# An encoder block on one core: the first gate/up pair from blocks 3 and 2, its operands made during the last output products, and attention products by array halves

## The chip, the core and the metric

The kernel runs on one core of a Trainium2 chip. TensorE (PE) multiplies: it holds a stationary operand of up to 128 x 128 in its array (loaded by PEld, beside a running product) and streams a moving operand through it into PSUM. VectorE (DVE), ScalarE (ACT) and GpSimd (POOL) do the rest, and SyncE (SP) issues most of the DMAs. The metric is the device time of one execution in microseconds. Three runs of the kernel before took 2155.74, 2158.10 and 2158.45 us, median 2158.1.

## The reference

One layer of a bidirectional encoder on x (1, 2048, 1024) in float32:

```
h   = RMSNorm(x);  p = h @ w_in                     q, k, v, g, two low-rank decays, u, z
A   = chunked gated linear attention, 4 heads (dk 64, dv 128), forwards and backwards
      scores = (q*exp(b)) (k*exp(-b))^T, masked;  o = scores v + (q*exp(b)) state
      o = RMSNorm(o) per head * silu(g)
Bm  = gelu(u) * (W_s LayerNorm(gelu(z)) + b)        per 128-token chunk and channel group
x   = x + concat(A, Bm) @ w_out
x   = x + (silu(h2 @ w_gate) * (h2 @ w_up)) @ w_down,   h2 = RMSNorm(x)
out = RMSNorm(x)
```

The hidden width of the last product is 2816, which is 22 tiles of 128.

## The kernel before, in words

The 2048 tokens are four blocks of 512 (b = 0 to 3). Every wide product is done in three passes: each float32 operand is split into a rounded part "h" (an ACT cast) and the remainder "l" (a DVE subtraction), and PE does h·h, h·l and l·h (L112 to L114, and L873 to L875). The small products of the attention are plain float32, each of which is two matmuls in the trace.

The stages in order of time. (1) Forward over blocks 0 to 3: projections of q, k and v, and the attention of the block before, put between those products. For each 128-token chunk `attend` makes the scores `sc` (L483: 8 products with contraction 64; first four for the heads in rows 0 to 63, then four for rows 64 to 127), transposes `kp`, the output `po` (four products with the masked scores, L512, and two with the state, L519, whose moving operand is a 128 x 256 state with zeros in the quarters that belong to the other head) and the state's increment `pd` (L527). (2) Backward over blocks 3 to 0: z, gate and u products, the backward attention `pob` (L693, again two products with a zero-filled 128 x 256 state), and the eight output products `pout`, whose sums become the block's residual stream x. While the next block's products run, `settle` and `norm2` turn x into h2 in place; blocks 3 and 2 are written to DRAM (`d_h`). (3) Gate and up products. Two blocks of tokens make a pair, and two tiles of hidden channels a set; each 2 x 2 product of a set is done with seven products of half the size instead of eight (Strassen-Winograd). Products 0 to 6 use seven moving operands held in `slots`, made by `moving` out of the pair's four quarters (b11, b21 of the first block and b12, b22 of the second) by `sub` (L237) and `put` (cast L226, remainder L227), and seven stationary operands, made for each set by `Stationary.job` out of two weight tiles (loads L302, sums L313, cast L334, remainder L335). `PAIRS` gives the pairs: (1, 0), then (3, 2). The gate's values go through a tanh into `cg`, the up products times `cg` go to DRAM (`d_a`). (4) The down products, block by block, and the last norm.

Engines run their queues in order; which instruction stands where on an engine is decided by a scheduler that works from the program's order, and a tile that reuses memory waits for the last reader of what was there. Around the change this matters at three places: the pair (1, 0) needs block 0, whose x is complete only with the last output product, and whose norm (`sums.rstd`, L194 to L196, and `norm_x0`, L837) comes before three of the operands; `tb` (operands 3 and 1) takes the buffer of `y`, the moving operand of the output products; and the pool `pf` of stage 3 takes the memory of the pool `pc` of stage 2.

Of the kernel before, what the change touches and what calls it, by code (L numbers as in the profile page):

```python
# [27 lines left out]
def encoder_block(  # L28
# [34 lines left out]
    mixer = ExitStack()  # L63
    mx = mixer.enter_context(tc.tile_pool(name="mx", bufs=1))
# [100 lines left out]
    rall = mx.tile([P, NB * TT], F32, tag="rall", name="rall")  # L165
# [54 lines left out]
    slots = {}  # L220

    def put(i, src, eng=nc.vector):
        hi, lo = slots[i]
        for k in range(0, HK, 2):
            c = slice(k, k + 2)
            nc.scalar.copy(out=hi[:, c, :], in_=src[:, c, :])  # L226
            eng.tensor_tensor(out=lo[:, c, :], in0=src[:, c, :], in1=hi[:, c, :].bitcast(F32), op=ALU.subtract)  # L227

    def moving(xa, xb, early=True, normed=None):


        b11, b21, b12, b22 = xa[:, 0:HK, :], xa[:, HK:KT, :], xb[:, 0:HK, :], xb[:, HK:KT, :]

        def sub(o, a, b, eng=nc.vector):
            for k in range(0, HK, 2):
                c = slice(k, k + 2)
                eng.tensor_tensor(out=o[:, c, :], in0=a[:, c, :], in1=b[:, c, :], op=ALU.subtract)  # L237

        if early:
            put(0, b11)  # L240
        if normed:
            normed(range(0, HK))
        sub(b11, b12, b11)
        put(3, b11)
        if early:
            put(4, b21)
        if normed:
            normed(range(HK, KT))
        sub(b11, b22, b11)
        put(1, b11)  # L250
        sub(b12, b22, b12, nc.gpsimd)
        put(6, b22, nc.gpsimd)
        put(2, b12)
        sub(b21, b21, b11)
        put(5, b21)
# [4 lines left out]
    d_h = {b: drp.tile([P, KT, TB], F32, tag=f"dh{b}", name=f"dh{b}") for b in (2, 3)}  # L260
# [4 lines left out]
    ech = mx.tile([P, 4, NB * TT * 2], F32, tag="ech", name="ech")  # L265
    dec = mx.tile([P, 4, NB * TT], F32, tag="dec", name="dec")
    gnh = mx.tile([P, 4], F32, tag="gnh", name="gnh")
# [8 lines left out]
    PAIRS = ((1, 0), (3, 2))  # L276
    TURNS = (0, NF // 2 - 1)
    STEADY = (0, 3, 4, 1, 2, 5, 6)

    class Stationary:  # L280


        def __init__(self):
            self.pool, self.n, self.two = None, 0, None
            sets = [(pair[0], p, which) for pair in PAIRS for p in range(NF // 2) for which in range(2)]
            self.made = [dict(of=s) for s in sets]

            jobs = []
            for i in range(0, len(sets), 2):
                jobs += ([(i + j, o) for o in STEADY for j in range(2)] if sets[i][1] in TURNS else  # L290
                         [(i + j, o) for j in range(2) for o in STEADY])
            self.stream = Stream([lambda j=j: self.job(*j) for j in jobs], ahead=4)

        def raw(self, i, r):
            if i < len(self.made) and r not in self.made[i]:
                b, p, which = self.made[i]["of"]
                name = f"w{'gu'[which]}{b}_{p}{'ab'[r]}"
                if (r == 0) if i < 2 else i % 2 == 0:
                    t = wp.tile([P, D], F32, tag="wraw", name=name, bufs=2)
                else:  # L300
                    t = self.pool.tile([P, D], F32, tag="raw", name=name, bufs=2)
                nc.sync.dma_start(out=t, in_=wgu[2 * p + r, which])  # L302
                self.made[i][r] = t
            return self.made[i].get(r) if i < len(self.made) else None

        def job(self, i, o):
            m = self.made[i]
            c1, c2 = slice(0, TB), slice(TB, D)
            ra = self.raw(i, 0)
            rb = self.raw(i, 1) if o not in (0, 4) else None  # L310
# [5 lines left out]
            if o == 3:  # L316
                m["s"] = self.pool.tile([P, TB], F32, tag="sum", name=f"sum{i}", bufs=2)
                src = into(m["s"], rb[:, c1], rb[:, c2], ALU.add)
            elif o == 1:
                src = into(m["s"], m["s"], ra[:, c1])  # L320
            elif o == 2:
                src = into(rb[:, c1], ra[:, c1], rb[:, c1])
            elif o == 6:
                src = into(m["s"], ra[:, c2], m["s"])
            else:
                src = {0: ra[:, c1], 4: ra[:, c2]}[o] if o != 5 else rb[:, c2]
            if o == 2:
                self.raw(i + 1, 0)
                self.raw(i + 1, 1)
# [5 lines left out]
            nc.vector.tensor_tensor(out=lo, in0=src, in1=hi.bitcast(F32), op=ALU.subtract)  # L335
            return hi, lo
# [4 lines left out]
    with tc.tile_pool(name="pa", bufs=1) as pa:  # L341
# [84 lines left out]
        sfs = [pa.tile([P, 2, 2, P], F32, tag=f"sf{i}", name=f"sf{i}") for i in range(2)]  # L426
        la = pa.tile([P, 2 * TT, 65], F32, tag="la", name="la")
        for z in (sfz, sbz, *sfs, la):
            nc.gpsimd.memset(z, 0.0)
# [44 lines left out]
        def attend(b, qd, kd, vs):  # L474
            for t in range(TT):
# [33 lines left out]
                po = small(f"po{g}")  # L509
                sf, sn = sfs[g % 2], sfs[(g + 1) % 2]  # L510
                for hd in range(4):
                    nc.tensor.matmul(out=po[:, hd * P:(hd + 1) * P], lhsT=s[:, hd, :], rhs=vs[t][:, hd, :],  # L512
                                     start=hd == 0, stop=g == 0 and hd == 3)
                if g > 0:
# [7 lines left out]
                nc.scalar.copy(out=ot, in_=po)  # L522
# [9 lines left out]
                if g + 1 < NB * TT:  # L532
                    for m in range(2):
                        for a in range(2):
                            r = slice(a * 64, (a + 1) * 64)
                            if g == 0:
                                nc.vector.tensor_copy(out=sn[r, m, a, :], in_=dsb[r, 2 * m + a, :])
                            else:
                                nc.vector.scalar_tensor_tensor(  # L539
                                    out=sn[r, m, a, :], in0=sf[r, m, a, :], scalar=dec[r, m, g:g + 1], in1=dsb[r, 2 * m + a, :],  # L540
# [69 lines left out]
    gfs = load([P, KT], gf, "gfs")  # L610
    with tc.tile_pool(name="pc", bufs=1) as pc:
# [22 lines left out]
        sbs = [pc.tile([P, 2, 2, P], F32, tag=f"sb{i}", name=f"sb{i}") for i in range(2)]  # L634
        for z in sbs:
            nc.gpsimd.memset(z, 0.0)
# [13 lines left out]
        def settle(b, xt):  # L650
# [4 lines left out]
            if b > 1:  # L655
# [4 lines left out]
        for b in range(NB - 1, -1, -1):  # L660
# [17 lines left out]
            def backward():  # L678
                for t in range(TT - 1, -1, -1):
# [6 lines left out]
                    if g < NB * TT - 1:  # L686
# [4 lines left out]
                        po = small(f"pob{g}")  # L691
                        for m in range(2):
                            nc.tensor.matmul(out=po[:, 2 * m * P:2 * (m + 1) * P], lhsT=qb[:, m, :],  # L693
                                             rhs=sb[:, m, :, :].rearrange("p a v -> p (a v)"), start=m == 0, stop=m == 1)
                        nc.vector.tensor_tensor(out=o, in0=po, in1=o, op=ALU.add)  # L695
                    for m in range(2):
                        for a in range(2):
                            r = slice(a * 64, (a + 1) * 64)
# [463 lines left out]
```

## Time and profile before

| | |
|---|---|
| three runs, median | 2158.1 us |
| profiled execution | 2151.09 us, span 2149.4 us |
| PE busy | 2092.1 us, 97% of the span, 9608 matmuls |
| PEld / DVE / ACT / POOL busy | 80% / 64% / 40% / 9% |
| mean granted clock of TensorE | 0.992 |
| DMA | 275.11 MB, mean 128 GB/s |

PE is busy nearly everywhere, so the time is the sum of its matmuls plus the places where it waits. The page's row of tenths finds these places; a table by windows sizes them, and the list of waits names what PE waited for. Starts and windows are in us from the start of the span. A matmul's duration is longer than its share of the time, since matmuls are pipelined: what one costs in a row is the distance from start to start.

### The profile page before, as it was taken

The page shows a single profiled execution, that of the slowest core. Times are in us where ns is not written, and L with a number is a line of the kernel's source. Part 1 is how long each engine was busy: PE and PEld are TensorE (multiplying, and loading weights), DVE is VectorE, ACT ScalarE, POOL GpSimd, SP SyncE. Part 2 cuts the span into 40 slices and gives each one's busy share as a digit, 9 for nine tenths or more (in the row PEclk, how much of TensorE's full clock was granted, in tenths as well). Part 3 has the DMA queues.
Part 4 walks back from the last instruction along what each step waited for, and adds up shares of the span by engine and source line. Part 5 has one row for each costly group of instructions (what it writes and reads, how often), then busy time and mean ns, then how long its engine had stood idle before and what let it go on. Part 6 is the DMA issues. An engine that isn't in the chain of part 4 may idle for free. (4 is left out here: it accounts for less than half of the span.)

```text
span 2149.4 us, 25584 instructions
## 1 busy us (share of the span) xinstructions
PE 2092.1 (97%) x9608; PEld 1726.4 (80%) x9608; DVE 1385.1 (64%) x2143; ACT 868.0 (40%) x1459; POOL 198.3 (9%) x276
## 2 busy tenths in 40 slices
PE   8999999999999968999999999999999999999998
PEld 6788887888888856888888878888888888888887
DVE  5977567676767668666666986666666445363633
ACT  6755455464636433323223433232324333333321
POOL 0122223010110120000000210000000000000000
PEclk9999999999999988999999999999999999999999
DMA  7633335353543324222222242222124537454531
GB/s 264 206 126 124 98 110 179 130 194 118 172 155 115 98 85 157 79 87 71 84 93 79 74 162 83 94 79 90 67 84 160 202 109 244 157 200 157 181 113 40
DMA packets 92812, 275.11 MB, mean 128 GB/s; under 512 B 11536, under 2 KB 19600, under 8 KB 90128
## 3 DMA queue, kind: packets, MB, share of 16 engines
q1 hardware_dynamic: 78960, 223.14, 31.2%
q0 software_dynamic: 13728, 50.34, 6.4%
q8 instruction: 75, 1.23, 0.2%
q14 instruction: 49, 0.40, 0.1%
HBM read 221.01 MB, written 52.43 MB: 127 GB/s over the span
## 5 line engine op out<-in xcount | busy, mean ns | idle before, releaser
L930 POOL DMA_DIRECT2D da<-q x88 | 47.6, 541 | 778.0 <-DVE q L929 759.0
L917 ACT ACTIVATE th<-cg 128x512 f32<-128x512 f32 x66 | 41.7, 632 | 140.0 <-DVE cg L915 130.0
L918 DVE SCALAR_TENSOR_TENSOR cg<-th,cg 128x512 f32<-128x512 f32 x66 | 45.5, 689 | 28.2 <-ACT th L917 28.0
L800 DVE TENSOR_TENSOR xc<-pout,xc 128x512 f32<-128x512 f32 x32 | 22.0, 689 | 49.9 <-PE pout L114 49.9
L929 DVE SCALAR_TENSOR_TENSOR q<-q,cg 128x512 f32<-128x512 f32 x66 | 47.4, 718 | 0.0
L995 POOL DMA_DIRECT2D out_dram<-xg x12 | 8.6, 716 | 368.4 <-DVE xg L992 367.8
L517 POOL TENSOR_SCALAR qs<-QK,ech 128x128 f32<-128x128 f32 x30 | 26.2, 876 | 162.4 <-PE po L519 84.4
L702 DVE SCALAR_TENSOR_TENSOR sb<-sb,dec,dsr 64x128 f32<-64x128 f32 x60 | 21.0, 350 | 28.6 <-PE pob L693 27.5
L539 DVE SCALAR_TENSOR_TENSOR sf<-sf,dec,dsb 64x128 f32<-64x128 f32 x56 | 19.5, 349 | 24.1 <-ACT dsb L529 23.4
L483 PEld LDWEIGHTS sc<-QK 64*128 64x128 f32 x256 | 24.5, 187 | 6.4 <-issue 4.9
L483 PE MATMUL sc<-QK 64*128 64x128 f32 x256 | 27.7, 285 | 0.8 <-DVE QK L469 0.8
L980 ACT CAST a_8h<-ar 128x512 fp32r<-128x512 f32 x32 | 18.7, 618 | 21.0 <-DMA ar<-da 20.9
L690 POOL TENSOR_SCALAR qb<-qb,ech 128x128 f32<-128x128 f32 x30 | 20.5, 691 | 72.5 <-DMA qb<-dq 71.6
L707 ACT ACTIVATE junk<-o 128x128 f32<-128x128 f32 x64 | 20.0, 312 | 16.0 <-DVE o L695 10.3
L522 ACT COPY ot<-po 128x512 f32<-128x512 f32 x16 | 9.4, 586 | 40.8 <-issue 23.9
L1067 DVE TENSOR_TENSOR xg<-pd,xg 128x256 f32<-128x256 f32 x16 | 6.8, 424 | 28.2 <-PE pd L114 27.8
L1039 DVE TENSOR_TENSOR xg<-pd,xg 128x512 f32<-128x512 f32 x24 | 16.6, 690 | 12.2 <-PE pd L114 12.2
L1069 ACT ACTIVATE lsq<-xg 128x256 f32<-128x256 f32 x16 | 6.7, 417 | 40.9 <-DVE xg L1067 40.9
L875 PE MATMUL g_0c<-tbh,op2l 128*128 128x512 f32 x4 | 2.6, 654 | 20.6 <-DVE op2l L335 20.6
L981 DVE TENSOR_TENSOR a_8l<-ar,a_8h 128x512 fp32r<-128x512 f32 x32 | 20.8, 680 | 2.6 <-ACT a_8h L980 2.5
L512 PEld LDWEIGHTS po<-v,s 128*128 128x128 f32 x128 | 15.6, 191 | 8.4 <-issue 8.2
L981 DVE TENSOR_TENSOR a_0l<-ar,a_0h 128x512 fp32r<-128x512 f32 x32 | 20.8, 686 | 2.0 <-ACT a_0h L980 1.8
(3826 smaller groups left out, 7392.5 us busy)
## 6 DMA issues: line engine op xcount, KB each, us to landing
wdn<-in_wdn_dram SPq DMA_DIRECT2D x88, 512.0 KB, 3.5
da<-q POOLq DMA_DIRECT2D x88, 256.0 KB, 2.5
ar<-da SPq DMA_DIRECT2D x88, 256.0 KB, 4.0
wo<-in_wo_dram SPq DMA_DIRECT2D x32, 512.0 KB, 3.6
wqk<-in_wqk_dram SPq DMA_DIRECT2D x16, 512.0 KB, 4.0
xk<-in_xtok_dram SPq DMA_DIRECT2D x16, 512.0 KB, 5.2
wv<-in_wv_dram SPq DMA_DIRECT2D x16, 512.0 KB, 3.5
xc<-in_xT_dram SPq DMA_DIRECT2D x4, 2048.0 KB, 9.6
```

Of the source, the lines that this page charges most:

```text
L483: nc.tensor.matmul(out=sc[a][:, i // 2, i % 2, :], lhsT=kd[i][r, c], rhs=qd[i][r, c], start=True, stop=True)
L517: nc.gpsimd.tensor_scalar_mul(qs[:, m, :], qd[m][:, c], ech[:, m, 2 * g:2 * g + 1])
L539: nc.vector.scalar_tensor_tensor(out=sn[r, m, a, :], in0=sf[r, m, a, :], scalar=dec[r, m, g:g + 1], in1=dsb[r, 2 * m + a, :], op0=ALU.mult ...
L690: nc.gpsimd.tensor_scalar_mul(qb[:, m, :], qb[:, m, :], ech[:, 2 + m, 2 * g + 1:2 * g + 2])
L702: nc.vector.scalar_tensor_tensor(out=sn[r, m, a, :], in0=sb[r, m, a, :], scalar=dec[r, 2 + m, g:g + 1], in1=ds_[r, m, :], op0=ALU.mult, op ...
L707: nc.scalar.activation(out=junk, in_=o[:, hd * P:(hd + 1) * P], func=AF.Square, scale=P ** -0.5, accum_out=va[:, 4 + 4 * t + hd:5 + 4 * t ...
L800: nc.vector.tensor_tensor(out=xt[:, n, :], in0=p, in1=xt[:, n, :], op=ALU.add)
L917: nc.scalar.activation(out=th, in_=a, func=AF.Tanh, scale=0.5)
L918: later.append(lambda: nc.vector.scalar_tensor_tensor(out=o, in0=th, scalar=1.0, in1=a, op0=ALU.add, op1=ALU.mult))
L929: nc.vector.scalar_tensor_tensor(out=q, in0=a, scalar=0.5, in1=cg[:, 2 * m + t, :], op0=ALU.mult, op1=ALU.mult)
L930: nc.gpsimd.dma_start(out=d_a[pair[t]][2 * p + m], in_=q)
L981: nc.vector.tensor_tensor(out=lo, in0=raw, in1=hi.bitcast(F32), op=ALU.subtract)
```

## The change

The pairs become (3, 2) and (1, 0). Blocks 3, 2 and now 1 go through DRAM as h2. During block 0's u products and output products block 3 is loaded into the buffer that block 1 had, and block 2 into a pool of its own (`ps6`); `moving`, now a generator of 22 steps of one cast and one subtraction, or of one subtraction, all on ACT and DVE and none on POOL, does 8 steps between the output products, and one after each of the first 14 gate/up products. Block 1 is loaded when operands 5 and 6 of the first pair are done, and block 0 gets its norm in set 3 of the first pair. The second pair's 22 steps begin after the first product of the first pair's last set. The order of the products in a set is 0, 4, 3, 1, 2, 6, 5, and a pair begins with products 0 and 4 of four sets (gate and up of the first two tile pairs), which need the first block's halves alone, and no sums of weights. The weight tiles are asked for by a list of first and last uses.

In the attention the score products alternate between rows 0 to 63 and rows 64 to 127. The state has no zero quarters any more: the products of `po` and `pob` with it are four of contraction 64 with 128 columns, alternating between the halves, and write to two PSUM tiles, one for each half, which two copies or two additions read.

```diff
-    PAIRS = ((1, 0), (3, 2))
-    TURNS = (0, NF // 2 - 1)
-    STEADY = (0, 3, 4, 1, 2, 5, 6)
+    PAIRS = ((3, 2), (1, 0))
+    STEADY = (0, 4, 3, 1, 2, 6, 5)
+    def sequence():
+        seq = []
+        for i in range(len(PAIRS)):
+            seq += [(i, p, w, o) for o in STEADY[:2] for p in range(2) for w in range(2)]
+            seq += [(i, p, w, o) for p in range(2) for o in STEADY[2:] for w in range(2)]
+            seq += [(i, p, w, o) for p in range(2, NP - 1) for w in range(2) for o in STEADY]
+            seq += [(i, NP - 1, w, o) for o in STEADY for w in range(2)]
+        return seq
...
-        sub(b11, b12, b11)
-        put(3, b11)
...
-        sub(b12, b22, b12, nc.gpsimd)
-        put(6, b22, nc.gpsimd)
...
+        yield from put(0, b11)
+        yield from sub(b11, b12, b11)
+        yield from put(4, b21)
+        yield from sub(b12, b22, b12)
+        yield from put(3, b11)
+        yield from sub(b11, b22, b11)
+        yield from put(1, b11)
+        yield from put(2, b12)
+        yield from put(6, b22)
+        yield from sub(b21, b21, b11)
+        yield from put(5, b21)
...
-                for a in range(2):
-                    r = slice(a * 64, (a + 1) * 64)
-                    for i in range(4):
+                for i in range(4):
+                    for a in range(2):
+                        r = slice(a * 64, (a + 1) * 64)
                         nc.tensor.matmul(out=sc[a][:, i // 2, i % 2, :], lhsT=kd[i][r, c], rhs=qd[i][r, c], start=True, stop=True)
...
-                        nc.tensor.matmul(out=po[:, 2 * m * P:2 * (m + 1) * P], lhsT=qs[:, m, :],
-                                         rhs=sf[:, m, :, :].rearrange("p a v -> p (a v)"), start=False, stop=m == 1)
+                        for a in range(2):
+                            r = slice(a * 64, (a + 1) * 64)
+                            nc.tensor.matmul(out=po[a][:, m, :], lhsT=qs[r, m, :], rhs=sf[r, m, :], start=False, stop=m == 1)
...
+                xa = xp.tile([P, KT, TB], F32, tag="x2", name="xf3")
+                xb = [ps6.tile([P, HK, TB], F32, tag=f"w{n}", name=f"xf2{n}") for n in range(2)]
...
+                operands = todo = moving(xa[:, 0:HK, :], xa[:, HK:KT, :], *xb)
...
-                drain(todo, 2)
-            drain(todo)
+                drain(todo, 2 if b else (1, 1, 1, 1, 2, 2)[n - 2])
...
-                if start:
+                whi, wlo = ws.next()
+                if start and ops.n <= 5:
+                    bank[key] = other(f"{name}{key}")
+                elif start:
                     bank[key] = psf.tile([P, TB], F32, tag="sp", name=f"{name}{key}", bufs=7)
...
+            if i == 0 and p < 2:
+                drain(operands, 1)
+            elif i == 0 and p == 2 and o == STEADY[0] and w == 0:
+                drain(operands)
+                x1 = xp.tile([P, KT, TB], F32, tag="x2", name="xf1")
+                nc.sync.dma_start(out=x1, in_=d_h[1])
+            elif i == 0 and p == 3:
+                drain(norm, 1)
+            elif n == at_end:
+                operands = moving(x1[:, 0:HK, :], x1[:, HK:KT, :], x0[:, 0:HK, :], x0[:, HK:KT, :])
+            elif n > at_end and done < 22 and (n - at_end - 1) * 0.8 >= done + 1:
+                drain(operands, 1)
+                done += 1
```

How PE's queue changes in one forward chunk (chunk 9; `sc`, `kp`, `po` and `pd` as above, `QK` the decayed q and k, `qs` the decayed q and `sf` the state). Before:

```order
L483 MATMUL sc9_0_2227<-QK_312 128x128 x4
L483 MATMUL sc9_1_2228<-QK_312 128x128 x4
L499 MATMUL kp9_2248<-ident_84,ke9_2243 128x128 x4
...
L512 MATMUL po9_2258<-v2_1_1773,s9_2241 128x128 x4
L519 MATMUL po9_2258<-sf1_305,qs9_2263 128x256 x2
L527 MATMUL pd9_2271<-v2_1_1773,kT9_2253 128x128 x4
```

The same chunk of the changed kernel (its line numbers are 24 to 26 higher):

```order
L507 MATMUL sc9_0_2254<-QK_305 128x128
L507 MATMUL sc9_1_2255<-QK_305 128x128
...
L523 MATMUL kp9_2275<-ident_81,ke9_2270 128x128 x4
...
L536 MATMUL po9_0_2285<-v2_1_1792,s9_2268 128x128
L536 MATMUL po9_1_2286<-v2_1_1792,s9_2268 128x128
...
L545 MATMUL po9_0_2285<-sf1_300,qs9_2291 128x128
L545 MATMUL po9_1_2286<-sf1_300,qs9_2291 128x128
...
L553 MATMUL pd9_2302<-v2_1_1792,kT9_2280 128x128 x4
```

The two score rows and the two state rows stand four times and twice, in turns between the halves. The `po` products with the state now lie between products that use all 128 rows.

On DVE, after the last output product (`pout0_7`), before: `r0` is block 0's norm factor, `xc0` and `xc1` the blocks' tiles, `tbl`, `s2l` and `s5l` remainders of moving operands, `op2l` the remainder of the first stationary operand of product 3.

```order
L800 TENSOR_TENSOR xc0_5386<-pout0_7_6591,xc0_5386 128x512
L186 TENSOR_TENSOR e0a_6335<-e0a_6335,e0sq7_6618 128x512
L196 RECIPROCAL r0_6621<-r0_6621 128x128 x4
L313 TENSOR_TENSOR sum0_6697<-wg1_0b_6695 128x512
L837 SCALAR_TENSOR_TENSOR xc0_5386<-xc0_5386,g2s_3005,r0_6621 128x512 x4
L237 TENSOR_TENSOR xc1_4437<-xc0_5386,xc1_4437 128x1024 x2
...
L237 TENSOR_TENSOR xc1_4437<-xc1_4437 128x1024 x2
L335 TENSOR_TENSOR op2l_6700<-sum0_6697,op2h_6699 128x512
```

The same place of the changed kernel, on DVE (`xf3`, `xf20` and `xf21` are the loaded blocks 3 and 2, `op2l` here the remainder for product 0 of the second tile pair, from the weight tile `wg0_1a`):

```order
L826 TENSOR_TENSOR xc0_5462<-pout0_7_6686,xc0_5462 128x512
L229 TENSOR_TENSOR tbl_6728<-xf3_6419,tbh_6727 128x1024
L186 TENSOR_TENSOR r0_6428<-r0_6428,e0sq7_6713 128x512
...
L239 TENSOR_TENSOR xf3_6419<-xf21_6421,xf3_6419 128x1024 x2
L229 TENSOR_TENSOR s2l_6730<-xf20_6420,s2h_6729 128x1024
L358 TENSOR_TENSOR op2l_6749<-wg0_1a_6738,op2h_6748 128x512
```

The reciprocals, the norm of block 0 and the long run of operand pieces no longer stand ahead of the first stationary remainder. What stands there now is one sum of squares (L186, the last reader of the pool that closes) and six pieces of operands, of which the second `tbl` is left out above.

## Rows read from the trace of the kernel before

**Rows 1.** The page: busy tenths of PE in 40 slices.

```profile
PE   8999999999999968999999999999999999999998
```

**Rows 2.** Windows: stretch, length, busy us (and instructions) by engine, PEclk, DMA share, GB/s.

```profile
200.00:300.00 100.00, 99.10 (x532) 82.20 (x531) 64.93 (x132) 56.46 (x108) 18.79 (x30) 1.00 0.29 96
900.00:1100.00 200.00, 200.00 (x884) 165.68 (x883) 134.27 (x212) 61.51 (x108) 10.81 (x20) 1.00 0.24 82
778.75:822.00 43.25, 17.00 (x55) 11.65 (x55) 40.35 (x38) 17.53 (x21) 12.64 (x5) 0.64 0.30 112
...
1235.00:1250.00 15.00, 11.62 (x51) 9.10 (x50) 15.00 (x15) 5.39 (x9) 5.14 (x3) 1.00 0.55 190
```

**Rows 3.** Waits of PE: line waited for, us in total, times, longest.

```profile
PE g_0c L875 <- DVE op2l L335: 20.6, 1, 20.6
...
PE g_0a L875 <- DVE op158l L335: 3.4, 1, 3.4
```

**Rows 4.** Timeline of DVE after the last output product: start, us, instruction.

```profile
783.03 3.39 DVE L196 RECIPROCAL r<-r 128x128 f32<-128x128 f32 x4 [1.94 <-ACT r L194]
...
798.81 6.65 DVE L237 TENSOR_TENSOR xc<-xc,xc 128x1024 f32<-128x1024 f32 x2
```

**Rows 5.** Timeline of PE there.

```profile
778.52 0.39 PE L114 MATMUL pout<-y0h,wo_7l 128*128 128x512 f32 x1
...
785.99 0.39 PE L875 MATMUL u_0a<-tah,op0l 128*128 128x512 f32 x1
788.19 0.50 PE L873 MATMUL g_0a<-tah,op4h 128*128 128x512 f32 x1 [1.81 <-ACT op4h L334]
...
815.08 0.80 PE L875 MATMUL g_0c<-tbh,op2l 128*128 128x512 f32 x1 [20.56 <-DVE op2l L335]
```

**Rows 6.** Windows of the granted clock around that wait.

```profile
788.00:790.00 2.00, 1.74 (x4) 0.80 (x4) 2.00 (x4) 0.66 (x2) 0.00 (x0) 0.68 0.00 0
...
815.00:819.50 4.50, 4.42 (x11) 3.49 (x12) 4.50 (x7) 1.13 (x2) 0.00 (x0) 0.51 1.02 419
```

**Rows 7.** Instructions of lines 226 and 227: minimum, median, maximum ns, first and last start.

```profile
L226 ACT CAST tah<-xf x4: 1049/1054/1056, 1195.5 to 1208.6; 128x1024 fp32r<-128x1024 f32 x4
...
L227 DVE TENSOR_TENSOR tal<-xf,tah x4: 1208/1214/1226, 1196.6 to 1215.6; 128x1024 fp32r<-128x1024 f32 x4
```

**Rows 8.** DMA issues: count, KB each, median us from issue to landing.

```profile
xf<-dh SPq DMA_DIRECT2D x2, 2048.0 KB, 8.7
...
wg_0b<-in_wgu_dram SPq DMA_DIRECT2D x2, 512.0 KB, 3.7
```

**Rows 9.** Timeline of ACT: one cast of a stationary operand.

```profile
787.00 0.62 ACT L334 CAST op2h<-sum 128x512 fp32r<-128x512 f32 x1
```

**Rows 10.** Timeline of PE, one chunk's scores.

```profile
252.91 0.39 PE L114 MATMUL pv<-wv_0h,n3l 128*128 128x512 f32 x1
253.23 1.71 PE L483 MATMUL sc<-QK 64*128 64x128 f32 x16
254.87 0.33 PE L499 MATMUL kp<-ident,ke 128*128 128x128 f32 x1
```

**Rows 11.** Weight loads of these scores in flight at 253.66 to 253.70, and at 254.00.

```profile
253.56 0.30 PEld L483 LDWEIGHTS sc<-QK 64*128 64x128 f32 x2
...
253.89 0.30 PEld L483 LDWEIGHTS sc<-QK 64*128 64x128 f32 x4
```

**Rows 12.** Timeline of PE, the same chunk's output, and a backward one.

```profile
257.88 1.13 PE L512 MATMUL po<-v,s 128*128 128x128 f32 x8
258.84 1.03 PE L519 MATMUL po<-sf,qs 128*128 128x256 f32 x4
259.71 0.50 PE L527 MATMUL pd<-v,kT 128*128 128x128 f32 x3
...
438.79 1.03 PE L693 MATMUL pob<-sb,qb 128*128 128x256 f32 x4
439.65 1.02 PE L193 MATMUL e3m<-e3a,ones 128*128 128x512 f32 x2
```

More of the change, by code (lines that the diff above doesn't have):

```diff
@@ L280, in encoder_block @@
     class Stationary:
         def __init__(self):
[L284 to L299, printed above, removed]
-                else:
[L301 to L310, printed above, removed]
+            self.pool, self.n, self.two, self.sums = None, 0, None, {}
+            self.seq = sequence()
+            self.loads, self.use = [], []
+            for n, (i, p, w, o) in enumerate(self.seq):
+                turn = p in (0, 1, NP - 1)
+                need = []
+                for r in ((0,) if o in (0, 4) else (1,) if o in (3, 5) else (0, 1)):
+                    key = (i, p, w, r, p == 1 and o in (0, 4))
+                    at = [l for l in self.loads if l["key"] == key]
+                    if not at:
+                        first = r == 0 if turn and not key[4] else False if key[4] else w == 0
+                        at = [dict(key=key, pool=not first, first=n)]
+                        self.loads += at
+                    at[0]["last"] = n
+                    need.append(at[0])
+                self.use.append(need)
@@ new lines, in __init__, with ask @@
+            self.queues = [[l for l in self.loads if l["pool"] == x] for x in (False, True)]
+            for q in self.queues:
+                for a, b in zip(q, q[2:]):
+                    assert a["last"] < b["first"]
+            self.asked = [0, 0]
+            self.stream = Stream([lambda n=n: self.job(n) for n in range(len(self.seq))], ahead=4)
+        def ask(self, done):
+            for x, q in enumerate(self.queues):
+                while self.asked[x] < len(q) and (self.asked[x] < 2 or q[self.asked[x] - 2]["last"] < done):
+                    l = q[self.asked[x]]
+                    i, p, w, r, _ = l["key"]
+                    pool, tag = (self.pool, "raw") if x else (wp, "wraw")
+                    l["tile"] = pool.tile([P, D], F32, tag=tag, name=f"w{'gu'[w]}{i}_{p}{'ab'[r]}", bufs=2)
+                    nc.sync.dma_start(out=l["tile"], in_=wgu[2 * p + r, w])
+                    self.asked[x] += 1
@@ L312, in into, with job @@
+        def job(self, n):
+            i, p, w, o = self.seq[n]
+            self.ask(n)
+            c1, c2 = slice(0, TB), slice(TB, D)
+            ra = rb = None
+            for l in self.use[n]:
+                if l["key"][3]:
+                    rb = l["tile"]
+                else:
+                    ra = l["tile"]
             def into(dst, a, b, op=ALU.subtract):
@@ L934, in encoder_block @@
         ws = ops.stream
-        for pair in PAIRS:
-            first = pair == PAIRS[0]
-            xa, xb = (x1, x0) if first else xs
-            moving(xa, xb, not first, norm_x0 if first else None)
-            for p in range(NP):
-                g, u = gate_set(p, pair), up_set(p, pair)
-                for x, i in ([(x, i) for i in STEADY for x in (g, u)] if p in TURNS else
-                             [(x, i) for x in (g, u) for i in STEADY]):
-                    x[i]()
-                if first and p == 2:
-                    xs = []
-                    for b in PAIRS[1]:
-                        xt = xp.tile([P, KT, TB], F32, tag="x2" if b % 2 else "x", name=f"xf{b}")
-                        nc.sync.dma_start(out=xt, in_=d_h[b])
-                        xs.append(xt)
+        sets = {}
+        seq = ops.seq
+        at_end = [n for n, (i, p, w, o) in enumerate(seq) if i == 0 and p == NP - 1][0]
+        norm, done = norm_x0(), 0
+        for n, (i, p, w, o) in enumerate(seq):
+            if (i, p, w) not in sets:
+                make = (gate_set, up_set)[w]
+                sets[i, p, w] = make(p, PAIRS[i])
+            sets[i, p, w][o]()
+            if i == 0 and p < 2:
[11 more added lines that the diff above has]
+                done += 1
             flush()
```

144 lines of the change are left out of this document (66 added, 78 removed).

## The prediction

> **What bounds the kernel now.** I read the page's row of tenths first: PE is at 9 nearly everywhere, and falls at the very start, in the middle (slices 14 and 15: "6" and "8") and at the end [rows 1]. So the time is PE's work and its holes. The table by windows gives the undisturbed rate: 884 matmuls in 200 us, 0.2265 us each [rows 2]. Then the middle hole: in the 43.25 us after the last output product PE has 55 matmuls [rows 2], which at 0.2265 are 12.5 us, so 31 us are lost. The list of waits names the owner of the largest part: 20.6 us for `op2l` on DVE [rows 3]. DVE's timeline shows what stands ahead of it: the four reciprocals run to 786.4, and a subtraction of operands is still at it at 805 [rows 4]; two of them take 6.65 us where a piece of this size takes 1.21 [rows 7], while POOL works on pieces of the same operands. PE's timeline shows the same from its side: two products at once, then 1.8 us, then small runs, and a restart at 815.08 [rows 5]. The clock is part of it: 0.68 and less after the first gap, 0.51 from 815 to 819.5, so eleven matmuls take 4.4 us instead of 2.5 [rows 6]; these 2 us are within the 31. A second, smaller hole stands where the pairs change: 15 us with 51 matmuls, so 3.4 us, all in one wait for `op158l` [rows 2, 3].
>
> **The change, part by part.**
>
> The large hole. Three things that filled it go: the first pair no longer needs block 0, so its sums, reciprocals and norm are off the path (set 3 has them, with DVE busy 134 of 200 us in such sets [rows 2]: 3.4 us of reciprocals [rows 4] and eight pieces of about 0.7 us fit the 12 us that 14 products leave free there). Eight of 22 steps move under the output products. The other 14 run under gate/up products, one to a product; products 0 and 4 of four sets give 8 x 12 matmuls x 0.2265 = 21.7 us in which only two moving operands, already made, are read.
>
> What is late next, in the times of before, with PE's output products done at 778.75 (start of the last, 778.52, and one distance [rows 5]). The first two products go on at once: their stationary parts are made before, the first has a PSUM bank outside the closing pool. They end at 778.75 + 24 x 0.2265 = 784.2. The third needs weight tile `wg0_1a`, loaded into the pool `pf`, which waits for the last reader of `pc`: the sum of channel 7's squares, row L186 of the new order. On DVE in front of it is the remainder `tbl`, whose cast cannot start before the last output product has read `y` (same buffer): 779.0 + 1.05 + 1.21 [rows 7] = 781.3, and the sum to 782. The DMA then lands 3.7 us later [rows 8], at 785.7, with its 0.33 us of issue at about 786, and the cast of 0.62 [rows 9] ends at 786.7. So a stall of 2.5 us, and some tenths for `op4h`, queued behind that cast, of which the next matmuls but two are made: 2.7. Its bounds: 0, if the pool opens at the residual; 8, if the load lands as late as the 8.7 us of a large one [rows 8]. It can pull the clock down: the gap of 2.2 us from 785.99 to 788.19 [rows 5] was followed by 0.68 [rows 6], while one of 3.4 us in the second hole left it at 1.00 [rows 2]. Another fall would cost the 2 us above; I take 0.8. Lost after: 3.5. Gain 31 - 3.5 = 27.5.
>
> DVE under the first sets. 28 products of 2.72 us are 76 us; DVE's usual share is 134/200, 51 us, and 14 steps of 1.21 are 17: 68 of 76. It fits, and the first eight products need few sums of weights, so the order starts with slack. `xf1`, 2 MB, stands on SP between the weight loads of the second tile pair and waits for operand 5; with 8.7 us to landing [rows 8] it is in before those weights are needed, by a few us. I take 0 for both; if the cover is gone, each missing step is 1.2 us of PE, 10 us in all.
>
> The second hole. Its 22 steps are spread at 0.8 to a product over 28 products, and the stationary parts of four sets' products 0 and 4 are made ahead of them. Gain 3.4, bounds 0 and 3.4.
>
> The attention. 46 groups change: 16 of scores, 15 of `po` and 15 of `pob` with the state. A scores group is 16 matmuls, 1.64 us from first to next (253.23 to 254.87) [rows 10]. That two halves can run side by side is in this trace: at 253.66, within the first half's products, two weight loads are in flight, and at 254.00, where the two halves meet, four [rows 11]. So alternating, 16 go as 8 pairs. Eight matmuls of 128 columns in one stream take 0.96 (257.88 to 258.84) [rows 12], and changing between full and half array costs the difference of 0.32 (252.91 to 253.23) [rows 10] and 0.23, 0.09, each way. The way in is ahead of the 1.64 both before and after, so the group becomes 0.96 + 0.09 = 1.05, and less the part that overlaps already I take 0.56 saved, 9 us in 16. A state group is now 4 matmuls of 256 columns, 0.87 (258.84 to 259.71, and 438.79 to 439.65) [rows 12]; it becomes 8 of 128 in 4 pairs, 0.48, and pays both ways, 0.18, and some start: 0.7, so 0.17 saved, 2.5 us in each of the two stages. Together 14. ACT gets a second copy for each chunk and DVE a second addition in place of one, both with a third of their time free; the halves write to two PSUM tiles, and these come free before the next chunk's scores ask for them, since a chunk lasts 10 us. Bounds: if the halves never ran together, 16 in a row would take 1.92 + 0.09 and a state group 0.96 + 0.18, so 16 x 0.37 + 30 x 0.27 = 14 us lost; if pairing were free of entry and start, all groups halve, 16 x 0.82 + 30 x 0.43 = 26 gained. I take 14, near the seam rows.
>
> The Trainium skill, "TensorEngine Tiling (Array Packing)", section Theoretical Speedup, gives up to 2x for a contraction of at most 64, which is the 26 of the upper bound and would make the time 2101; its section Key Properties says that a change of tiling mode drains the engine, which speaks against the state groups, each between products of the full array. The 0.09 each way [rows 10] is what this trace shows of that.
>
> Sum: 27.5 + 3.4 + 14 = 45 us. The profiled execution is 2151.09 (span 2149.4), and becomes 2106; the runs' median is 7 us higher, and the holes are the same in kind there: 2158 - 45 = 2113.
>
> **The rivals.**
>
> 1. The halves do not pay: PE keeps program order between them, or each change costs more than 0.09. For it: the products in turns are pairs of matmuls of one half, since a float32 product is two. Against: four loads in flight at the seam. With the bound of 14 lost, 2158 - 31 + 14 = 2141; with no effect, 2127.
> 2. DVE becomes the bound in the first sets, and PE waits there for operand 3, 2, 6 or 5 or for sums of weights. For it: 68 of 76 us, and a queue in order, with evacuations between the pieces. Against: products 0 and 4 come first. 10 us: 2123.
> 3. The hole is not closed but moved: the third product waits for its weight tile as long as 8 us, with the clock down: 2113 + 7 = 2120. It goes with 2.
> 4. The full halving of all 46 groups: 2101.
> 5. Slower: the groups of half-array matmuls, now shorter and denser, let the granted clock fall as it did after the gap at 786. The price of one fall is the 2 us of 815 to 819.5 [rows 6]; 46 of them are 92, and the time 2158 - 31 + 92 = 2219. It decides from 31/46 = 0.67 us a group. Against it: 16 groups with contraction 64 are in the kernel already, and the stretch 200 to 300, which holds several, has 1.00 [rows 2].
>
> **How the numbers follow.** The sum as it stands, 2107 to 2119: 0.63. Rival 1: 0.12, half of it above 2131. Rivals 2 and 3: 0.15, 2117 to 2130. Rival 4: 0.06. Rival 5 and anything else that ends slower: 0.04. Range 2104 to 2131, predicted 2113. A difference under 0.2% (4.3 us) cannot be told from none here. Faster by more 0.95, within 0.02, slower 0.03.
>
> **What would show it.** In the new profile: no DVE-bound wait above 4 us after the output products, and one wait of 2 to 3 us after 24 gate/up matmuls, ended by ACT's cast of a weight tile; slices at 9 in the middle; windows over the first 28 gate/up products with under 2 us lost; no wait where the pairs change; 1.0 to 1.1 us from the first score matmul to `kp`, with four weight loads in flight all along; about 0.7 for a state group. Wrong would be: score groups at 1.6 or more, waits of PE for DVE spread over the first 76 us of gate/up, or a clock under 1.00 in the attention.

## The result, and the profile after

The changed kernel takes 2130.05 us (2127.53 to 2132.07, 4 runs), the kernel before beside it 2157.52 us (2155.74 to 2158.45, 4 runs): ratio 0.9881, 95% interval 0.9867 to 0.9895. It is faster by 27.5 us, and not by 45. The profiled executions have spans of 2149.4 and 2125.8 us, 23.6 apart; the profiled execution of before, 2151.09, lies 6.4 us under the median beside it, that of the changed kernel, 2127.53, 2.5 under its own. From the 2158.1 of the forecast the ratio makes 2132.4, just above the end of the range, 2131.

The holes are closed. The page of the kernel after, busy tenths of TensorE and its granted clock in 40 slices, which answer to [rows 1]:

```profile
PE   8999999999999999999999999999999999999998
PEclk9999999999999999999999999999999999999999
```

No slice in the middle is under 9. The windows say the same in counts, and something else too. Columns as in [rows 2]; the second row is the 43.25 us after the last output product, the third the pair change, the fourth lies in the attention:

```profile
900.00:1100.00 200.00, 199.85 (x872) 161.91 (x871) 136.56 (x215) 62.24 (x106) 10.80 (x20) 1.00 0.23 82
778.48:821.73 43.25, 41.43 (x183) 33.84 (x182) 39.77 (x53) 22.91 (x34) 1.98 (x4) 1.00 0.44 165
1216.00:1231.00 15.00, 15.00 (x68) 12.43 (x67) 14.57 (x22) 7.00 (x11) 1.08 (x2) 1.00 0.74 248
200.00:300.00 100.00, 97.09 (x549) 78.95 (x549) 65.28 (x132) 56.58 (x113) 18.42 (x30) 1.00 0.29 99
```

183 matmuls stand where 55 stood, 68 where 51 stood. But the steady stretch has 872 in 200 us, where [rows 2] has 884, although both say busy 200: twelve matmuls of 0.2265 us, 2.7 us, are gone there without TensorE being idle. That is in no term of the forecast.

TensorE's waits in the kernel after (line waited for, us in total, times, longest):

```profile
PE po L536 <- DVE s L513: 9.9, 15, 2.8
...
PE g_1a L902 <- ACT op2h L357: 1.8, 1, 1.8
```

The 20.6 and the 3.4 us of [rows 3] are gone. The stall that the forecast put in their place is there, a quarter shorter than worked out. TensorE's timeline (start, us, instruction, idle time before it and its releaser):

```profile
783.69 0.39 PE L904 MATMUL u_0a<-tah,op0l 128*128 128x512 f32 x1
785.91 0.50 PE L902 MATMUL g_1a<-tah,op2h 128*128 128x512 f32 x1 [1.82 <-ACT op2h L357]
```

2.22 us from start to start, so 2.0 lost, with the granted clock at 1.00 all through in this trace. The other wait of the list is new in size: the output `po` waits 9.9 us for the scores `s`, in 15 chunks. Before it was 3.1 us in 4:

```profile
PE po L512 <- DVE s L489: 3.1, 4, 1.8
```

**Where the 45 went.** The matmuls behind the last output product, which starts at 778.52 before and at 778.25 after, can be counted off in both traces. The 100th starts at 832.42 before and 803.09 after, the 1,700th at 1195.09 and 1170.85, the 2,000th (behind the pair change) at 1266.93 and 1238.85, the 3,700th (the end of gate/up) at 1652.26 and 1628.66. Counted from the last output product, 0.27 earlier after, the changed kernel is ahead by 29.1, 24.0, 27.8 and 23.3 us: this is called the lead below. Against the forecast's terms:

| term | forecast, us | trace, us |
|---|---|---|
| large hole | 27.5 | 29.1 |
| pair change | 3.4 | 3.8 |
| attention, first scores to last output product | 14 | 3.6 |
| gate/up behind the large hole and behind the pair change | 0 | -5.1 and -4.5 |
| ahead of the first scores (79.72 before, 83.01 after) | 0 | -3.3 |
| behind gate/up | 0 | 0.0 |

They sum to 23.6, the distance of the two spans. Two terms are wrong: the attention, and the gate/up products behind the holes, which the forecast took as unchanged. Experiment 1 asks whether the -3.3 belongs to the change.

**The chunk.** TensorE's timeline of the same chunk as in [rows 10, 12], in the kernel after:

```profile
255.17 1.16 PE L507 MATMUL sc<-QK 64*128 64x128 f32 x16
256.26 0.66 PE L523 MATMUL kp<-ident,ke 128*128 128x128 f32 x4
...
259.80 1.13 PE L536 MATMUL po<-v,s 128*128 128x128 f32 x8 [0.38 <-DVE s L513]
260.86 0.71 PE L545 MATMUL po<-sf,qs 64*128 64x128 f32 x8
261.51 1.16 PE L553 MATMUL pd<-v,kT 128*128 128x128 f32 x8
262.42 0.48 PE L111 MATMUL pv<-wv_1l,n3h 128*128 128x512 f32 x1
```

The scores take 1.09 us where they took 1.64, as forecast. And from the first score to the output it is 4.63 us, where it was 4.65 (253.23 to 257.88 in [rows 10, 12]). VectorE shows why, first before, then after (start, us, instruction):

```profile
254.42 0.45 DVE L486 COPY_PREDICATED sfz<-fm,sc 128x256 f32<-128x256 int32 x1 [2.21 <-PE sc L483]
254.76 0.44 DVE L486 COPY_PREDICATED sbz<-bm,sc 128x256 f32<-128x256 int32 x1
255.09 1.22 DVE L89 TENSOR_TENSOR wv_3l<-wv,wv_3h 128x1024 fp32r<-128x1024 f32 x1
256.23 0.45 DVE L486 COPY_PREDICATED sfz<-fm,sc 128x256 f32<-128x256 int32 x1
...
257.04 0.69 DVE L489 TENSOR_TENSOR s<-sfz,sbz 128x512 f32<-128x512 f32 x1
```

```profile
256.36 1.23 DVE L87 TENSOR_TENSOR wv_3l<-wv,wv_3h 128x1024 fp32r<-128x1024 f32 x1 [2.19 <-ACT wv_3h L86]
257.50 0.45 DVE L510 COPY_PREDICATED sfz<-fm,sc 128x256 f32<-128x256 int32 x1
257.83 0.45 DVE L510 COPY_PREDICATED sbz<-bm,sc 128x256 f32<-128x256 int32 x1
...
258.97 0.69 DVE L513 TENSOR_TENSOR s<-sfz,sbz 128x512 f32<-128x512 f32 x1
```

Before, the first half of the scores was whole early, and two of the four masked copies began while TensorE worked on the second half. In turns, both halves become whole together at the end; all four copies come after it, and behind the remainder of a weight. These six instructions, four copies, the remainder and the sum, begin 1.19 us after the first score and take 3.3 us in both kernels, so `s` is ready 4.5 us after the first score in both.

**The steady products.** TensorE's timeline at the start of a steady set, then the weight load and ScalarE's copy that belong to it:

```profile
859.93 0.39 PE L904 MATMUL g_2a<-tah,op28l 128*128 128x512 f32 x1
860.16 0.39 PE L902 MATMUL g_2c<-tbh,op30h 128*128 128x512 f32 x1
...
860.84 0.39 PE L902 MATMUL g_2c<-tbh,op30h 128*128 128x512 f32 x1
861.07 0.44 PE L902 MATMUL g_2a<-tah,op28h 128*128 128x512 f32 x1
861.34 0.40 PE L903 MATMUL g_2a<-tal,op28h 128*128 128x512 f32 x1
```

```profile
861.00 0.19 PEld L902 LDWEIGHTS g_2a<-tah,op28h 128*128 128x128 f32 x1 [0.19 <-ACT u2g L913]
```

```profile
860.36 0.59 ACT L913 COPY u2g<-g_2a 128x512 f32<-128x512 f32 x1 [1.74 <-PE g_2a L904]
```

Product 0 has left `g_2a`; ScalarE copies it out until 860.95; product 4 adds to the same bank, and only 4 matmuls of product 3 stand between. Its first weight load waits until 861.00, and TensorE takes 0.273 us for one step in place of 0.227. A bank is here the PSUM tile that a product is summed in. This is the diff's `STEADY`: (0, 3, 4, 1, 2, 5, 6) became (0, 4, 3, 1, 2, 6, 5). Products 0 and 4 share bank a; product 6 adds to bank c, which VectorE reads after product 2. One product, 12 matmuls, stood between the two of each pair, and now they are neighbours. Over the 32 steady sets the distances from start to start add up to 8.7 us more than the undisturbed ones; most of the other 0.9 us of the two gate/up terms is lost ahead of them, in the first two tile pairs. None of it is in TensorE's list of waits, but it is in that of its weight loads:

```profile
PEld g_4c L902 <- DVE cg L944: 0.9, 2, 0.6
...
PEld u_7a L902 <- ACT u2u L913: 0.5, 2, 0.3
```

### The profile page after: what moved, and what is told of

It reads as the page before. It is cut to its first block, busy times and chain, and to the rows that moved or that the text cites. A ratio compares the mean times of both kernels' runs of the same rounds, so it can differ in the third digit from the quotient of the medians.

```text
span 2125.8 us, 25829 instructions
## 1 busy us (share of the span) xinstructions
PE 2088.7 (98%) x9728; PEld 1705.8 (80%) x9728; DVE 1362.1 (64%) x2134; ACT 871.8 (41%) x1475; POOL 169.3 (8%) x266
## 3 DMA queue, kind: packets, MB, share of 16 engines
q1 hardware_dynamic: 79968, 227.33, 31.5%
## 4 chain that ended last, share of the span: by engine, by line
PE 88%; DVE 5%; ACT 3%; DMA 3%; issue 1%; SPq 0%; POOL 0%; DVEq 0%; ACTq 0%; POOLq 0%
PE pd L110 8%; PE pd L111 8%; PE pd L112 8%; PE pout L112 3%; PE pout L111 3%; PE pout L110 3%; PE pu L110 1%; PE pu L111 1%; PE pu L112 1%; PE pz L110 1%; PE pz L111 1%; PE pg L110 1%; PE pg L111 1%; PE pz L112 1%; PE pg L112 1%
## 5 line engine op out<-in xcount | busy, mean ns | idle before, releaser
L541 POOL TENSOR_SCALAR qs<-QK,misc 128x128 f32<-128x128 f32 x30 | 24.9, 833 | 164.5 <-PE po L545 83.6
L565 DVE SCALAR_TENSOR_TENSOR sf<-sf,misc,dsb 64x128 f32<-64x128 f32 x56 | 19.8, 354 | 23.9 <-ACT dsb L555 23.2
L731 DVE SCALAR_TENSOR_TENSOR sb<-sb,misc,dsr 128x128 f32<-128x128 f32 x30 | 9.9, 345 | 33.8 <-PE pob L721 33.0
L548 ACT COPY ot<-po 128x256 f32<-128x256 f32 x32 | 10.3, 376 | 46.1 <-issue 23.4
L536 PE MATMUL po<-v,s 128*128 128x128 f32 x128 | 18.1, 284 | 9.9 <-DVE s L513 9.9
L716 POOL TENSOR_SCALAR qb<-qb,misc 128x128 f32<-128x128 f32 x30 | 18.9, 640 | 78.1 <-DMA qb<-dq 66.5
L1103 DVE TENSOR_TENSOR xg<-pd,xg 128x256 f32<-128x256 f32 x16 | 6.8, 424 | 28.2 <-PE pd L112 27.8
L375 ACT ACTIVATE xk<-xk 128x1024 f32<-128x1024 f32 x16 | 17.0, 1063 | 13.8 <-DMA xk<-in_xtok_dram 13.8
L1017 DVE TENSOR_TENSOR a_0l<-ar,a_0h 128x512 fp32r<-128x512 f32 x32 | 20.6, 686 | 1.0 <-ACT a_0h L1016 1.0
L507 PEld LDWEIGHTS sc<-QK 64*128 64x128 f32 x256 | 15.6, 187 | 6.5 <-issue 5.3
```

The costliest lines, as they stand in the source:

```text
L536: nc.tensor.matmul(out=po[hd % 2][:, hd // 2, :], lhsT=s[:, hd, :], rhs=vs[t][:, hd, :], start=hd < 2, stop=g == 0 and hd > 1)
L541: nc.gpsimd.tensor_scalar_mul(qs[:, m, :], qd[m][:, c], ech[:, m, 2 * g:2 * g + 1])
L565: nc.vector.scalar_tensor_tensor(out=sn[r, m, :], in0=sf[r, m, :], scalar=dec[r, m, g:g + 1], in1=dsb[r, 2 * m + a, :], op0=ALU.mult, op1= ...
L1017: nc.vector.tensor_tensor(out=lo, in0=raw, in1=hi.bitcast(F32), op=ALU.subtract)
```

## The experiments

Each was timed in 5 rounds against the kernel before; the first four ran together (before 2156.84 us), and the last four (2157.33 us). Spans are of the profiled execution.

**1. The changed kernel again.** No edit.

> The changed kernel once more, as the measure for the three beside it and for one open place: its trace reached the first group of scores at 83.01 us, the trace of before at 79.72, though neither has a changed instruction on TensorE ahead of it. Theory A, the 3.3 us belong to that one execution (a granted clock of 0.83 from 40 to 50 us, loads that landed later): the first group comes at 79.5 to 81.5 us and the span is 2 to 3 us under 2125.8. Theory B, they belong to the change: 82.5 to 83.5 again and a span within 1 us. The ratio to before should be 0.987 to 0.990 in either case.

2128.09 us, ratio 0.9870 (0.9853 to 0.9888), span 2126.0. The first scores came at 80.6 us, and the first `po` at 88.4, later than the 87.7 of the first trace: what was early was lost at once. So neither theory came out whole. In the six other traces that follow with the scores' start in its old place the first scores came between 82.5 and 85.2 us. So this place differs by some us between executions. The 79.7 of before is the earliest of all, but there is one trace of that kernel; whether the change has a part in it stays open.

This trace shows one thing more. The stall after 24 gate/up matmuls is 2.51 us from start to start here, and the granted clock falls behind it, to 0.50, the lower of its two levels (1.2 GHz); length and columns as in [rows 2]:

```profile
786.00:788.00 2.00, 2.00 (x6) 1.54 (x6) 1.79 (x3) 2.00 (x5) 0.00 (x0) 0.50 0.00 0
```

Six matmuls stand in 2 us here, and eight in a row are late. The first 28 products lose 4.7 us in this trace and 2.8 in the first. Of the six traces with this stall, the one of experiment 7 shows the same fall, and the other four have 1.00 there.

**2. The steady products in their old order.**

```
-  seq += [(i, p, w, o) for p in range(2, NP - 1) for w in range(2) for o in STEADY]
+  seq += [(i, p, w, o) for p in range(2, NP - 1) for w in range(2) for o in (0, 3, 4, 1, 2, 5, 6)]
```

> The changed kernel with the products of the steady tile pairs (2 to 9 of each block pair) in the order of before, 0 3 4 1 2 5 6, in place of 0 4 3 1 2 6 5; the first two and the last tile pair stay as they are. Theory A: the 9 us that the kernel loses between the first products and the end of gate/up against before (29.1 us ahead at 100 products' matmuls, 24.0 at the pair change; 27.85 after it, 23.4 at the end) are waits at reused PSUM banks: product 4 adds to bank a one product (2.7 us, of which the order on TensorE makes 4 or 5 matmuls) after product 0 left it, and waits for ScalarE's copy of it, product 6 on bank c likewise for VectorE's sum. With the old order there are two products between, so 8 to 9 us less than the changed kernel, ratio to before 0.9840 plus or minus 0.0015, and windows of 200 us in the steady part with 883 or 884 matmuls. Rival B: the losses come from where the operands 0 and 6 now lie, or from the VectorE load, not from the order: the same 0.988, with 875 matmuls in such a window.

2122.01 us, ratio 0.9840 (0.9825 to 0.9856), 6.1 us under the changed kernel beside it; the span is 2116.7, 9.3 less. The same window, 900 to 1100:

```profile
900.00:1100.00 200.00, 200.00 (x882) 165.30 (x881) 140.97 (x222) 63.55 (x108) 10.81 (x20) 1.00 0.24 81
```

882 in place of 872. The lead over before is 27.8 us from the 700th matmul to the 1,900th and 31.5 from the 2,300th to the 3,700th: nothing is lost in the steady part any more. At the 3,700th the changed kernel had 23.3, so 8.2 of the 9.6 us come back; the other 1.4 are lost ahead of the 700th and just behind the pair change. No weight load waits for `cg` or `u2` in the list. Theory A holds; the loss was the order.

**3. The scores in their old order.**

```
-  for i in range(4):
-      for a in range(2):
+  for a in range(2):
+      for i in range(4):
```

> The changed kernel with the sixteen matmuls of a chunk's scores in the order of before (all of one half of the array, then all of the other); all else stays, the states by halves too. Theory A: between scores and output TensorE waits for VectorE's chain (four masked copies, one remainder of a weight, one sum), which takes the same 4.6 us from the first score in both kernels; so a score group of 1.64 in place of 1.09 us costs nothing: the wait for s falls from 9.9 us to 2 to 4, the time stays within 2 us of the changed kernel. Rival B, the forecast's: the 16 x 0.55 us count, and the kernel is 8 to 9 us slower, ratio to before 0.992.

2130.33 us, ratio 0.9881 (0.9864 to 0.9899), 2.2 us over the changed kernel beside it. The same chunk:

```profile
258.87 1.71 PE L507 MATMUL sc<-QK 64*128 64x128 f32 x16
260.51 0.66 PE L523 MATMUL kp<-ident,ke 128*128 128x128 f32 x4
263.52 1.13 PE L536 MATMUL po<-v,s 128*128 128x128 f32 x8
```

Scores 1.64 us, and 4.65 to the output: the same time, although the scores take half as long again. The wait for `s` is 4.9 us in 4 chunks, 3.7 of them in one; it, and the 2.2 us, lie just outside of what theory A gave, the 2.2 within the interval. From the fifth scores to the last it takes 164.4 us, the changed kernel 163.8, the kernel before 164.9: eleven groups that are 0.55 shorter, 6 us of work, are worth 0.6. Theory A in substance, and not the 8 to 9 us.

**4. A whole product between scores and output.**

```
-                drain(att, 0 if i == 0 else 2)
+                drain(att, 1 if i == 0 else 2)
...
                 if i == 0:
-                    drain(att, 2)
+                    drain(att, 1)
...
-            drain(att, (0, 2, 2, None)[hd])
+            drain(att, (1, 2, 2, None)[hd])
```

> The changed kernel with a whole product (24 matmuls, 5.4 us) between a chunk's scores and its output: the first step of the attention of a block goes one product earlier, and of each two steps drained at a product the first is the output of the chunk before, the second the scores of the next. Theory A (the chain of 4.6 us on VectorE sets when the output may start): the 9.9 us of waits for s go to under 2, and the forward stage becomes 6 to 9 us shorter, ratio to before 0.984 to 0.9855. Rival B: VectorE is the limit of that stage as a whole (seven to nine tenths busy), the wait moves to the transposes, to the state or to the operands of the next block, and under 2.5 us are gained. Rival C: the scores of a block's first chunk now wait for its queries and keys, and this costs more than 2 us.

2135.06 us (2128.57 to 2141.83), ratio 0.9903 (0.9885 to 0.9921): slower than the changed kernel by 7 us. Waits of TensorE:

```profile
PE sc L507 <- DVE QK L493: 8.2, 4, 2.7
...
PE po L536 <- DVE s L513: 1.0, 1, 1.0
```

The wait for `s` is all but gone, as theory A had it, and rival C took its place: the first scores of each block, now a product earlier, wait for their queries and keys. The profiled span, 2126.9, is 1 us longer than that of the changed kernel, but the timed runs spread over 13 us. Their granted clocks go with it, 0.998 in the fastest and 0.992 in the slowest; what lowers the clock isn't shown, and so not what part of the 7 us is the waits.

**5. The attention by halves alone, on the kernel before.** The scores, `po` and `pob` with their tiles and copies as in the diff's part on attention, and nothing else of it.

> The kernel before with the attention by array halves alone (scores, po and pob as in the changed kernel; nothing else). Theory A: the halves run side by side (scores 1.09 in place of 1.64 us, po with its state 1.71 in place of 1.83, pob with its way in 0.96 in place of 0.91), but between scores and output VectorE's chain sets the pace, so the forward stage from the first scores to the last output is 0 to 3 us shorter and the ratio to before 0.9985 to 1.0005. Rival B, the forecast's term: 14 us, ratio 0.9935. Theory C: the change of attention costs time by itself, through the second copies on ScalarE and VectorE: above 1.001.

2154.16 us, ratio 0.9987 (0.9978 to 0.9997): 2.8 us gained, 0.6 to 4.7 by the interval. The same chunk, and the wait:

```profile
256.78 1.16 PE L483 MATMUL sc<-QK 64*128 64x128 f32 x16
...
261.41 1.13 PE L512 MATMUL po<-v,s 128*128 128x128 f32 x8 [0.35 <-DVE s L489]
262.47 0.71 PE L521 MATMUL po<-sf,qs 64*128 64x128 f32 x8
```

```profile
PE po L512 <- DVE s L489: 9.6, 15, 2.9
```

4.63 us again. The wait belongs to the halves and not to the other parts of the change. Theory A.

**6. The early weight tiles in the tile of the gates.**

```
-  l["tile"] = pool.tile([P, D], F32, tag=tag, ...)
+  if i == 0 and l["key"][4]:
+      if self.spare is None:
+          self.spare = gp.tile([P, 4, TB], F32, tag="g", name="spare")
+      l["tile"] = self.spare[:, 2 * w:2 * w + 2, :].rearrange("p a c -> p (a c)")
+  else:
+      l["tile"] = pool.tile([P, D], F32, tag=tag, ...)
```

The gate's own `cg` tile is then made at its first use.

> The changed kernel with the two weight tiles for products 0 and 4 of the second tile pair loaded into the tile of the gates, free since the last gated output, in place of the pool that opens after the last output product. Theory A: the stall after the first 24 gate/up matmuls (2.0 us, ended by ScalarE's cast of that weight) goes, and nothing takes its place: 2 us less, which is 0.1% and at the limit of what the times tell; the trace must have no start-to-start distance above 0.5 us in the first 100 gate/up matmuls. Rival B: the next thing that is late (a remainder of the operand for product 3, or the sum of weights) takes 1 us or more of it back there or within the next 14 products.

2126.44 us, ratio 0.9859 (0.9842 to 0.9876). The stall is gone from the list, and no distance from start to start between 770 and 860 us is above 0.3; after 400 matmuls the lead is 31.1 us, where the changed kernel has 28.4 in its first trace and, with the fall of the clock, 26.4 in that of experiment 1. Theory A. The 1.7 us in the times agree with it, but lie within the interval.

**7. The output later in three of four chunks.**

```
-                drain(att, 0 if i == 0 else 2)
+                drain(att, (0, 1, 2, 2)[i])
...
                 if i == 0:
-                    drain(att, 2)
+                    drain(att, 3)
...
-            drain(att, (0, 2, 2, None)[hd])
+            drain(att, (0, 1, 2, None)[hd])
```

> The changed kernel with a whole product between scores and output for three of a block's four chunks; the scores of the first chunk stay where they are (so their queries and keys are as early as now), and the last chunk's output follows its scores after 7 matmuls. Theory A: the waits for s go at twelve chunks (0.4 to 0.5 us each), the last of each block waits 1 to 1.5 us, no scores wait for queries or keys: 1 to 4 us less from the first scores to the last output (240 us now), ratio to before 0.9855 to 0.988. Rival B: the chain on VectorE then makes the transposes or the next block's operands late, and nothing is gained or some us are lost, as with the whole shift.

2126.36 us, ratio 0.9858 (0.9843 to 0.9874). The waits:

```profile
PE po L536 <- DVE s L513: 5.1, 5, 1.3
...
PE sc L507 <- ACT ot L548: 2.4, 4, 0.9
```

From the first scores to the last output 236.4 us, in the changed kernel 239.9 in experiment 1: 3.5 gained, as theory A had it. Scores that now wait for the copy of the output just ahead of them take back some of it. In the times it is 1.7 us, within the interval.

**8. 2, 6 and 7 together.**

> The steady products in the order of before, the early weight tiles in the free tile of the gates, and three of four outputs a product later, together. If the three causes are separate, they add: 9 and 2 and 1 to 4 us, so 12 to 15 us under the changed kernel, ratio to before 0.980 to 0.983. If the gaps share a cause, less than 9.

2116.01 us (2114.32 to 2118.56), ratio 0.9813 (0.9797 to 0.9828): 12.1 us under the changed kernel's 2128.09, 41 under before, and the fastest here. Its steady window, 900 to 1100, has 882 matmuls again. The lead is 30.8 us through the first pair, from the 700th matmul, and 34.4 through the second: both holes closed, and nothing given back in the steady part. The 12.1 us lie at the lower end of what the expectation gave for three separate causes. The three alone gained 6.1, 1.7 and 1.7 us, 9.5 together; the times agree with causes that add, within their intervals, but don't show it closely.

## Why the prediction was wrong

- **What bounds the kernel, and the large hole: right.** 29.1 us where 27.5 stood. The stall came after 24 matmuls, released by ScalarE's cast of the weight; it cost 2.0 and not 2.7. That the 0.8 for the clock wasn't needed is luck of this trace: experiment 1, the same kernel, has the fall.
- **VectorE under the first sets: right, with nothing to spare.** It was busy 10.00 of 10 us from 790 to 800, and TensorE still had its 46 matmuls.
- **Pair change: right**, 3.8 for 3.4.
- **"16 go as 8 pairs … I take 0.56 saved, 9 us in 16": the step that failed.** The group was measured as forecast, 0.55 saved. But the sum took a group's length for the chunk's. It asked whether the PSUM tiles come free, and never followed the scores to their reader: four masked copies, a remainder of a weight and a sum on VectorE, 4.5 us from the first score, with `po` right behind. TensorE's list of before held the clue, a wait of `po` for `s` of 3.1 us, and it wasn't read. Experiments 3 and 5 show it from both sides. In place of the forecast's 14 the attention gained 3.6.
- **The state groups: the size.** The forecast put 0.17 saved on each of 30, from the distance to the next start alone. That distance is shorter, 1.83 to 1.71 us for `po` with its state (1.06 and 0.65 above), and longer where the group stands between wide products, way in and group: 0.23 and 0.68 before, 0.318 and 0.645 after. But the products right behind the group don't stand at the same distances in the two kernels, so the count has to go on to where both run alike. For `po` that is the wide product behind `pd`: 257.88 to 260.52 before, 259.80 to 262.42 after, 2.64 and 2.62 us.

```profile
260.52 0.48 PE L112 MATMUL pv<-wv_1h,n3h 128*128 128x512 f32 x1
```

For `pob` (11 of 15 are like this one; the 0.87 of [rows 12] has `e3m`, matmuls of another kind, behind it) it is the third product after it, counted from the last one ahead. TensorE's timeline of such a group, before and then after:

```profile
425.90 0.40 PE L114 MATMUL pz<-wz_0h,c2l 128*128 128x512 f32 x1
426.14 1.03 PE L693 MATMUL pob<-sb,qb 128*128 128x256 f32 x4
426.81 0.58 PE L112 MATMUL pz<-wz_1h,c2h 128*128 128x512 f32 x1
...
427.46 0.39 PE L114 MATMUL pz<-wz_1h,c2l 128*128 128x512 f32 x1
```

```profile
426.37 0.39 PE L112 MATMUL pz<-wz_0h,c2l 128*128 128x512 f32 x1
426.69 0.72 PE L721 MATMUL pob<-sb,qb 64*128 64x128 f32 x8
427.34 0.50 PE L110 MATMUL pz<-wz_1h,c2h 128*128 128x512 f32 x1
...
427.91 0.40 PE L112 MATMUL pz<-wz_1h,c2l 128*128 128x512 f32 x1
```

1.56 us before and 1.54 after. So a state group of either kind saves 0.02 to 0.03 us, under 1 us in all 30, where 5 were forecast. (The expectation of experiment 5 reads a loss of 0.05 for `pob` out of the distance to the next start; it isn't one.)
- **The term that was missing: the steady order.** The diff moves product 4 ahead of 3 and product 6 ahead of 5 in the steady sets, to which the prediction gave no term. It is 8.7 us in the trace; experiment 2 gives 8.2 back there, and 6 in the times.
- **The rivals.** The time came out as in rival 1, 2127 to 2141, but not by its cause: the halves do run together. Rival 4 would have needed score groups of 0.82. Rivals 2 and 3 didn't occur. Nor did rival 5, as a fall with each group: the clock stood at 1.00 from 200 to 300 us in every trace. Single falls in the attention are in some traces (experiment 3: 0.83 from 100 to 110 us), with old and new order of the scores alike; the one trace of the kernel before has none there.

## What to carry to other kernels

A group that becomes shorter is worth what its reader lets through: follow the result to the next instruction of the same engine that needs it, and time that chain first. When an order of products is changed, look for two that share a bank, and count what stands between the read-out of the first and the start of the second. And compare counts of matmuls in equal windows, not busy shares: a busy engine hid eight microseconds here, which stood in the waits of the weight loads. And price a group of another shape up to where the products behind it run at their old pace, not up to the next start.

## What was not expected of the hardware

A wait for a bank that is ready within a few tenths of a microsecond hardly showed as idle time of the matmuls: busy stayed at 199.85 of 200 us while 12 of 884 matmuls were lost. And a pair of half-array matmuls of 128 columns follows the one before in 0.11 us, yet a group of four pairs takes 0.645 (260.86 to 261.51): the first pair and the way out cost 0.1 each beyond that spacing, and the first full-array matmul behind it 0.1 again (0.21 to the next, where before it was 0.11). So eight half-array matmuls of 128 columns in place of four full ones of 256 are here about where the change of shape pays for itself: 0.02 us saved. A stall of 2.2 to 2.5 us between gate/up matmuls was followed by a fall of the granted clock to 0.50 in two of six traces and by none in four.
